# Attention: weights' gains and low parts, and the norm of keys and queries, on GpSimd; V's copies out of PSUM on ScalarE

## The chip, the core and the metric

The kernel runs on one core of one Trainium2 chip. A core has five engines that run side by side, each through its own list of instructions: TensorE (PE in the profile; its weight loads are PEld), VectorE (DVE), ScalarE (ACT), GpSimd (POOL) and SyncE (SP), which issues the DMAs here. They wait for one another by semaphores. The metric is the time of one execution on the device, in microseconds (us); less is better.

## What is computed

A trunk of two layers on 1024 tokens of width 1024, in float32. Layer one is a Mamba-2 mixer, layer two an attention mixer with 16 heads of 64; each is followed by a gated embedding. The change touches the attention alone. Cut to that, and with its helpers' names, the reference says:

```python
kv = rmsnorm(h, norm_g) @ w_kv
k = rmsnorm(kv[..., :SB_WIDTH].reshape(bsz, s, SB_HEADS, SB_HEAD_DIM), k_g)
v = kv[..., SB_WIDTH:].reshape(bsz, s, SB_HEADS, SB_HEAD_DIM)
...
qg = rmsnorm(h, norm_g) @ w_in
q = rmsnorm(qg[..., :SB_WIDTH].reshape(bsz, s, SB_HEADS, SB_HEAD_DIM), q_g)
z = jnp.einsum('bhtd,bhsd->bhts', q, k)
weights = jnp.where(strict, jnp.exp(jax.nn.log_sigmoid(z) + suffix), 0.0)
o = jnp.einsum('bhts,bhsd->bhtd', weights, v)
return (o * jax.nn.silu(gate)) @ w_out
```

`suffix` is the running sum of log_sigmoid(-z) over the later keys of a strictly causal row, and `rmsnorm` divides by the root of the mean square. The kernel holds the tokens in reverse order, turns the sums of logarithms into running products of sigmoid(-z), and weights the differences of neighbouring rows of V with them.

## The kernel before, in words

**Precision.** A product of float32 matrices is made of three products of rounded parts: each operand is split into a high part (rounded) and a low part (the remainder). `hilo` (line 99) makes the two: the high part on ScalarE (L104), and the low part either on GpSimd (L106, without a gain) or in one operation on VectorE that also multiplies by a gain (L108).

**Pairs of heads.** Attention works on eight pairs of heads, `hp` = 0 to 7. `Pairs.load` (line 752) fetches a pair's weights in four transfers of 128x1024 (L758) and splits each into four pieces of 128x256: two of key and value columns, with the gain `kvn`, and two of query and gate columns, with `sn`. So a pair has 16 pieces. The weights of the next pair are made while the present one runs.

**Steps.** A pair has four steps, p = 3, 2, 1, 0, of two blocks of 128 tokens each. `step(i)` (line 992) writes out TensorE's order by hand, from three steps at once: it projects step i (`project`, 48 matmuls, and `gate` for p = 3 and 2), with pieces of the two steps before it in between: `flip` and `scores` of step i-1, `turn` and `product` of step i-2. The flip stands at half of step i's projections. All other engines' orders come from the framework's planner, which takes the instructions as the program issues them and puts each on its engine when it expects its operands to be ready, the earlier issued first.

**What a step does around the change.** `project` (line 812) leaves key, value and query of a block in PSUM; L825 copies key and query out on ScalarE, L826 the value on VectorE. When both blocks are done, `step` calls `values` and then `norm` (lines 1028 and 1029).

`values` (line 843) needs V shifted by one row: L847 to L849 move it from partition to partition by DMA from SyncE's queue, L852 fetches its first rows. Then GpSimd subtracts (L853) and makes high and low parts for the two heads (L858, L859, twice each).

`norm` (line 861) squares key and query on ScalarE (L864), sums over 64 on VectorE (L867), forms the mean (L85), guesses the inverse root by integer operations (L74, L75), refines it three times (L77, L78, L79: three operations each, on 128x8) and multiplies key and query by it (L870, 128x512), all on VectorE. `flip` (line 873) transposes the result on TensorE (L879), and L885 to L890 split it for `scores`.

Of the kernel before, what the change touches and what calls it, by code (L numbers as in the profile page):

```python
# [8 lines left out]
F32 = mybir.dt.float32  # L9
F32R = mybir.dt.float32r  # L10
BF16 = mybir.dt.bfloat16
I32 = mybir.dt.int32
AF = mybir.ActivationFunctionType
ALU = mybir.AluOpType
# [4 lines left out]
P = 128  # L19
# [10 lines left out]
EPS = 1e-6  # L30
# [18 lines left out]
def split3_some(nc, out, pairs, m):  # L49

    n = len(pairs)
    for i, (a, b) in enumerate(pairs):
        nc.tensor.matmul(out, lhsT=a, rhs=b, start=(i == 0), stop=(i == n - 1))  # L53
        if i % m == m - 1 and i < n - 1:
            yield


def terms(a, b):
    return [(a[0], b[0]), (a[0], b[1]), (a[1], b[0])]
# [530 lines left out]
class PleWeights:  # L590
# [7 lines left out]
    def load(self, pool, n):  # L598

        k, layer = self.k, self.layer  # L600
        for kk in (0, 2, 4, 6, 8):
            src, j, out = (self.A["gate"], kk, self.gates) if kk < 8 else (self.A["proj"], 0, self.projs)
            raw = self.rawp.tile([P, 1024], F32, name="raw").rearrange("p (r c) -> p r c", c=512)
            k.nc.sync.dma_start(raw, src[layer, j * P:(j + 2) * P, n * 512:n * 512 + 512].rearrange("(r p) c -> p r c", p=P))
            for r in range(2):
                hi = pool.tile([P, 512], F32R, name=f"g{n}h")
                lo = pool.tile([P, 512], F32R, name=f"g{n}l")
                k.hilo(hi, lo, raw[:, r], k.plen[:, layer, kk + r:kk + r + 1] if kk < 8 else 0.5)
                out[j + r][n] = (hi, lo)
            yield  # L610
# [133 lines left out]
class Pairs:  # L744
# [7 lines left out]
    def load(self, hp):  # L752

        k = self.k
        st = self.sts[hp] = {"W": [], "hp": hp}
        for q in range(4):
            raw = self.rawp.tile([P, 1024], F32, name="raw")
            k.nc.sync.dma_start(raw, self.A["w_b"][hp, :, q * 1024:(q + 1) * 1024])  # L758
            pool, bufs = (self.pool, 10) if hp == 0 or (4 * hp + q) % 6 != 3 else (self.more, 2)
            for i in range(2):  # L760
                hi = pool.tile([P, 512], F32R, name="g0h", bufs=bufs)
                lo = pool.tile([P, 512], F32R, name="g0l", bufs=bufs)
                for m in range(2):
                    g = (k.kvn if m == 0 else k.sn)[:, 2 * q + i:2 * q + i + 1]
                    sl = slice(m * 256, m * 256 + 256)
                    k.hilo(hi[:, sl], lo[:, sl], raw[:, i * 512 + m * 256:i * 512 + m * 256 + 256], gain=g)
                st["W"].append((hi, lo))
            yield

# [14 lines left out]
def attention(k, A, rawp, hT, oTd, dbg, b2, pairs):  # L784


    tc, nc = k.tc, k.nc
# [3 lines left out]
    with ExitStack() as ctx:  # L791
        pp = ctx.enter_context(tc.tile_pool(name="b_pair", bufs=1, reuse_waits="tile"))
        wk = ctx.enter_context(tc.tile_pool(name="b_work", bufs=2, reuse_waits="tile"))
        sm = ctx.enter_context(tc.tile_pool(name="b_small", bufs=2, reuse_waits="tile"))
        zp = ctx.enter_context(tc.tile_pool(name="b_z", bufs=2, space=PSUM, reuse_waits="tile"))
        trp = ctx.enter_context(tc.tile_pool(name="b_tr", bufs=2, space=PSUM, reuse_waits="tile"))
        op = ctx.enter_context(tc.tile_pool(name="b_o", bufs=2, space=PSUM, reuse_waits="tile"))
# [14 lines left out]
        def project(st, b):  # L812
            W = st["W"]
            ps = mm.tile([P, 512], F32, name="mm")
            prs = []
            sl = slice(b % 4 * P, b % 4 * P + P)
            for kk in range(KT):
                whi, wlo = W[kk]
                prs += terms((hh[b // 4][:, kk, sl], hl[b // 4][:, kk, sl]), (whi[:, :384], wlo[:, :384]))
            yield from split3_some(nc, ps[:, :384], prs, 6)  # L820
            p = b // 2
            if b % 2:
                st["kq"] = wk.tile([P, 2, 2, P], F32, name="kq", bufs=2)
                st["vr"][p] = wk.tile([P, 2, P], F32, name="vr", bufs=3)
            nc.scalar.copy(st["kq"][:, b % 2], ps.rearrange("p (m c) -> p m c", c=256)[:, :, 0:128])  # L825
            nc.vector.tensor_copy(st["vr"][p][:, b % 2], ps[:, 128:256])  # L826
            yield

        def gate(st, half):
# [31 lines left out]
        def norm(st, p):  # L861
            kq = st.pop("kq")
            sq = wk.tile([P, 512], F32, name="sg", bufs=1)
            nc.scalar.activation(sq, kq.rearrange("p b m c -> p (b m c)"), AF.Square)  # L864
            n = 8
            ss = sm.tile([P, n], F32, name="kss")
            nc.vector.reduce_sum(ss, sq.rearrange("p (g d) -> p g d", d=64), axis=AX.X)  # L867
            y = k.rstd(sm, ss, n, 64, EPS, "kr")
            x = kq.rearrange("p b m (h d) -> p (b m h) d", d=64)
            nc.vector.tensor_tensor(x, x, y.unsqueeze(2).broadcast_to([P, n, 64]), op=ALU.mult)  # L870
            st["kn", p] = kq

        def flip(st, p):
# [98 lines left out]
        n = len(steps)  # L972
# [19 lines left out]
        def step(i):  # L992
# [12 lines left out]
            if i < n:  # L1005
                hp, p = steps[i]
                if p == NT // 2 - 1:
                    pairs.all(hp)
                    begin_pair(sts[hp])
                    if hp + 1 < 8:  # L1010
                        pairs.start(hp + 1)
                    else:
                        b2.begin(pairs)
                fill = [(project(sts[hp], 2 * p + 1), 5)]
                if p >= 2:
                    fill.append((gate(sts[hp], p - 2), 7))
                fill.append((project(sts[hp], 2 * p), 5))
# [7 lines left out]
            if i < n:  # L1025
                if p in LOADS:
                    pairs.step(hp + 1)
                values(sts[hp], p)
                norm(sts[hp], p)
                if i in CHUNKS:  # L1030
                    b2.weights(CHUNKS[i])
# [228 lines left out]
```

## Time and profile before

| | |
|---|---|
| median of three runs | 1833.93 us (1831.68 to 1837.17) |
| the profiled execution's own time | 1837.69 us |
| its span in the trace | 1836.0 us |
| TensorE busy | 1725.0 us, 94% of the span |
| VectorE, ScalarE, GpSimd busy | 1189.7, 894.6, 402.2 us |
| attention stage | from about 930 to about 1600 us of the span |

The span is what the trace covers; the own time has the start and the end of the execution around it. Busy time counts an engine's instructions, not its waits. In the views, a line such as L853 is the line of the kernel that issued the instruction, `out<-in` are the program's tiles, and what stands behind "<-" at the end of a row is what ended the idle time ahead of it. SPq is the queue of SyncE that issues DMAs: its duration is that of the issue, not of the transfer. The granted clock is the share of TensorE's full clock that it was given, 1.00 being 2.4 GHz and 0.50 being 1.2 GHz.

### The profile page before, as it was taken

How to read it: one execution, taken by the hardware profiler on the slowest of the kernel's cores; microseconds unless marked ns; L12 is line 12 of the kernel's file. 1: busy time of each engine (PE TensorE's matmuls, PEld its weight loads, DVE VectorE, ACT ScalarE, POOL GpSimd, SP SyncE). 2: the span in 40 equal slices, each digit the busy share in tenths (PEclk: the TensorE clock that was granted, in tenths of full speed). 3: DMA queues.
4: the chain of work that ended last, by engine and by line, in shares of the span. 5: the costliest groups of instructions: out<-in, count | busy, mean ns of one | idle time of the engine just before them, and what ended most of it. 6: DMA issues, size and time to landing. Idle time of an engine off the chain costs nothing.

```text
span 1836.0 us, 25269 instructions
## 1 busy us (share of the span) xinstructions
PE 1725.0 (94%) x9170; PEld 1452.7 (79%) x9170; DVE 1189.7 (65%) x2462; ACT 894.6 (49%) x1910; POOL 402.2 (22%) x448
## 2 busy tenths in 40 slices
PE   7999999999999999999998999899999998689999
PEld 6777877877876787888887888788888887578887
DVE  6687278279169554345658797887878787962332
ACT  6567359349337332124436564564646554641221
POOL 0234534524625122200001011111101011210110
PEclk9999999999999999999999999999999999899999
DMA  4223213213212754322212010101111012232110
GB/s 155 66 81 91 82 62 94 90 60 99 92 52 87 238 160 149 118 97 78 94 40 65 19 54 19 52 31 39 44 29 65 19 44 74 87 118 69 51 38 35
DMA packets 96397, 139.42 MB, mean 76 GB/s; under 512 B 18160, under 2 KB 66640, under 8 KB 96272
## 3 DMA queue, kind: packets, MB, share of 16 engines
q1 hardware_dynamic: 96272, 137.80, 23.4%
q8 instruction: 72, 1.18, 0.3%
q14 instruction: 53, 0.43, 0.1%
HBM read 108.77 MB, written 24.77 MB: 73 GB/s over the span
## 4 chain that ended last, share of the span: by engine, by line
PE 67%; DVE 20%; ACT 7%; DMA 3%; issue 2%; POOL 0%; SPq 0%; DVEq 0%; ACTq 0%
PE mm L46 40%; PE mm L53 12%; DVE pt L910 6%; PE pq L46 2%; PE oq L942 2%; DVE v L234 2%; PE intra L409 2%; DVE g0l L108 1%; PE tr L922 1%; DVE wl L932 1%; PE inter L404 1%; ACT pt L908 1%; PE tr L664 1%; DMA raw<-in_gate 1%; PE tr L925 1%
## 5 line engine op out<-in xcount | busy, mean ns | idle before, releaser
L46 PE MATMUL mm<-ul,wh 128*128 128x512 f32 (+1 forms) x648 | 254.0, 392 | 0.0
L46 PE MATMUL mm<-uh,wh 128*128 128x512 f32 (+1 forms) x648 | 252.6, 390 | 0.8 <-ACT v L232 0.7
L46 PE MATMUL mm<-uh,wl 128*128 128x512 f32 (+1 forms) x648 | 252.5, 390 | 0.0
L53 PE MATMUL mm<-g0h,hh 128*128 128x384 f32 x512 | 182.7, 357 | 0.0
L910 DVE TENSOR_TENSOR_SCAN pt<-pt,keep 128x128 f32<-128x128 f32 (+7 forms) x128 | 177.0, 1386 | 0.8 <-ACT pt L908 0.3
L53 PE MATMUL mm<-g0l,hh 128*128 128x384 f32 x512 | 172.8, 337 | 2.4 <-DVE g0l L108 2.4
L53 PE MATMUL mm<-g0h,hl 128*128 128x384 f32 x512 | 172.9, 338 | 0.0
L234 DVE SCALAR_TENSOR_TENSOR v<-u,convh,v 128x512 f32<-128x512 f32 x144 | 129.4, 904 | 53.5 <-ACT v L232 51.0
L931 ACT CAST wh<-tr 128x512 fp32r<-128x512 f32 (+1 forms) x160 | 86.9, 544 | 154.8 <-PE tr L925 154.0
L853 POOL TENSOR_TENSOR vs<-vs,vr 128x256 f32<-128x256 f32 x32 | 24.1, 754 | 550.3 <-DMA vs<-vr 319.1
L46 PEld LDWEIGHTS mm<-uh,wh 128*128 128x128 f32 x648 | 121.7, 188 | 26.9 <-ACT v L232 1.6
L46 PEld LDWEIGHTS mm<-ul,wh 128*128 128x128 f32 x648 | 121.7, 188 | 26.3 <-issue 2.3
L46 PEld LDWEIGHTS mm<-uh,wl 128*128 128x128 f32 x648 | 121.8, 188 | 25.8 <-issue 1.9
L932 DVE TENSOR_TENSOR wl<-tr,wh 128x512 fp32r<-128x512 f32 (+1 forms) x160 | 101.5, 635 | 43.8 <-ACT wh L931 41.6
L106 POOL TENSOR_TENSOR wl<-raw,wh 128x1024 fp32r<-128x1024 f32 x39 | 95.3, 2444 | 157.6 <-ACT wh L104 150.9
L922 PE MATMUL tr<-ident,pt 128*128 128x128 f32 x320 | 75.4, 284 | 31.5 <-DVE wl L932 28.9
L574 DVE SCALAR_TENSOR_TENSOR acc<-mm,rg,acc 128x512 f32<-128x512 f32 x64 | 47.8, 749 | 84.9 <-PE mm L46 83.5
L53 PEld LDWEIGHTS mm<-g0l,hh 128*128 128x128 f32 x512 | 96.9, 189 | 4.0 <-DVE g0l L108 3.0
L906 PE MATMUL z<-kst,qh 128*128 128x320 f32 (+3 forms) x192 | 72.9, 380 | 27.9 <-ACT pt L908 15.8
L53 PEld LDWEIGHTS mm<-g0h,hh 128*128 128x128 f32 x512 | 96.6, 189 | 1.0
L53 PEld LDWEIGHTS mm<-g0h,hl 128*128 128x128 f32 x512 | 96.4, 188 | 0.0
L647 DVE SCALAR_TENSOR_TENSOR pth<-pth,pq 128x512 f32<-128x512 f32 (+1 forms) x33 | 22.2, 672 | 113.8 <-PE pq L46 109.1
(350 smaller groups left out, 4356.8 us busy)
## 6 DMA issues: line engine op xcount, KB each, us to landing
raw<-in_w_in SPq DMA_DIRECT2D x40, 512.0 KB
ex<-acd SPq DMA_DIRECT2D x64, 256.0 KB
raw<-in_w_b SPq DMA_DIRECT2D x32, 512.0 KB
raw<-in_m_out SPq DMA_DIRECT2D x16, 512.0 KB
raw<-in_gate SPq DMA_DIRECT2D x16, 512.0 KB
graw<-gT SPq DMA_DIRECT2D x30, 256.0 KB
gT<-zs SPq DMA_DIRECT2D x28, 256.0 KB
acc<-in_x SPq DMA_DIRECT2D x8, 512.0 KB
```

Of the source, the lines that this page charges most:

```text
L46: nc.tensor.matmul(out, lhsT=a, rhs=b, start=(i == 0), stop=(i == n - 1))
L53: nc.tensor.matmul(out, lhsT=a, rhs=b, start=(i == 0), stop=(i == n - 1))
L106: (eng or nc.gpsimd).tensor_tensor(lo, raw, hi.bitcast(F32), op=ALU.subtract)
L234: nc.vector.scalar_tensor_tensor(vv, u[:, 3 - j:3 - j + 512], w(j), vv, op0=ALU.mult, op1=ALU.add)
L409: nc.tensor.matmul(aq[hp * 64:hp * 64 + 64, jp * 256 + i * P:jp * 256 + (i + 1) * P], lhsT=xdts[2 * qt + i][:, (2 * j + hp) * 64:(2 * j + ...
L574: nc.vector.scalar_tensor_tensor(acc[:, sl], ps, k.rg[:, g, t:t + 1], acc[:, sl], op0=ALU.mult, op1=ALU.add)
L906: nc.tensor.matmul(z[:, :n], lhsT=qh[:, h, qs], rhs=rk, start=True, stop=False)
L910: nc.vector.tensor_tensor_scan(pt[:, :N], pt[:, :N], keep[:, :N], 1.0, op0=ALU.mult, op1=ALU.max)
L922: nc.tensor.transpose(tq[:, c:c + P], al[:, i0:i0 + P], ident)
L931: nc.scalar.copy(wh[:, :c], tq[:, :c])
L932: nc.vector.tensor_tensor(wl[:, :c], tq[:, :c], wh[:, :c].bitcast(F32), op=ALU.subtract)
L942: nc.tensor.matmul(out[:, :w], lhsT=st["V"][j // 2][:, j % 2, h * P:(h + 1) * P], rhs=rhs, start=(j0 == 2 * p and i == 0), stop=(j0 == NT ...
```

## The change

Three parts. For pairs 1 to 7 a piece of the weights is first multiplied by its gain in place on GpSimd, and then split without a gain: high part on ScalarE, low part on GpSimd instead of VectorE. Pair 0 is left as it was. The copy of V out of PSUM goes to ScalarE. In the norm the three refinements, written as four operations each, and the product with key and query go to GpSimd; mean and first guess stay on VectorE.

```diff
@@ -763,7 +763,12 @@
                 for m in range(2):
                     g = (k.kvn if m == 0 else k.sn)[:, 2 * q + i:2 * q + i + 1]
                     sl = slice(m * 256, m * 256 + 256)
-                    k.hilo(hi[:, sl], lo[:, sl], raw[:, i * 512 + m * 256:i * 512 + m * 256 + 256], gain=g)
+                    x = raw[:, i * 512 + m * 256:i * 512 + m * 256 + 256]
+                    if hp == 0:
+                        k.hilo(hi[:, sl], lo[:, sl], x, gain=g)
+                    else:
+                        k.nc.gpsimd.tensor_scalar(x, x, g, None, op0=ALU.mult)
+                        k.hilo(hi[:, sl], lo[:, sl], x)
                 st["W"].append((hi, lo))
             yield
 
@@ -823,7 +828,7 @@
                 st["kq"] = wk.tile([P, 2, 2, P], F32, name="kq", bufs=2)
                 st["vr"][p] = wk.tile([P, 2, P], F32, name="vr", bufs=3)
             nc.scalar.copy(st["kq"][:, b % 2], ps.rearrange("p (m c) -> p m c", c=256)[:, :, 0:128])
-            nc.vector.tensor_copy(st["vr"][p][:, b % 2], ps[:, 128:256])
+            nc.scalar.copy(st["vr"][p][:, b % 2], ps[:, 128:256])
             yield
 
         def gate(st, half):
@@ -865,9 +870,17 @@
             n = 8
             ss = sm.tile([P, n], F32, name="kss")
             nc.vector.reduce_sum(ss, sq.rearrange("p (g d) -> p g d", d=64), axis=AX.X)
-            y = k.rstd(sm, ss, n, 64, EPS, "kr")
+            v, y, r = (sm.tile([P, n], F32, name=x) for x in ("krv", "kry", "krs"))
+            nc.vector.tensor_scalar(v, ss, 1.0 / 64, EPS, op0=ALU.mult, op1=ALU.add)
+            nc.vector.tensor_single_scalar(y.bitcast(I32), v.bitcast(I32), 1, op=ALU.logical_shift_right)
+            nc.vector.tensor_scalar(y.bitcast(I32), y.bitcast(I32), -1.0, float(0x5F3759DF), op0=ALU.mult, op1=ALU.add)
+            for _ in range(3):
+                nc.gpsimd.tensor_tensor(r, y, v, op=ALU.mult)
+                nc.gpsimd.tensor_tensor(r, r, y, op=ALU.mult)
+                nc.gpsimd.tensor_scalar(r, r, -0.5, 1.5, op0=ALU.mult, op1=ALU.add)
+                nc.gpsimd.tensor_tensor(y, r, y, op=ALU.mult)
             x = kq.rearrange("p b m (h d) -> p (b m h) d", d=64)
-            nc.vector.tensor_tensor(x, x, y.unsqueeze(2).broadcast_to([P, n, 64]), op=ALU.mult)
+            nc.gpsimd.tensor_tensor(x, x, y.unsqueeze(2).broadcast_to([P, n, 64]), op=ALU.mult)
             st["kn", p] = kq
 
         def flip(st, p):
```

## Rows read from the trace of the kernel before

**Rows 1.** The page, busy time of TensorE: us, share of the span, instructions.

```profile
PE 1725.0 (94%) x9170; PEld 1452.7 (79%) x9170; DVE 1189.7 (65%) x2462; ACT 894.6 (49%) x1910; POOL 402.2 (22%) x448
```

**Rows 2.** Windows, one pair each: us, PE, PEld, DVE, ACT, POOL busy, clock, DMA.

```profile
1152.36:1234.04 81.68, 75.12 (x456) 68.57 (x456) 67.50 (x151) 46.75 (x107) 9.42 (x20) 1.00 0.13 39
1234.04:1318.45 84.41, 77.80 (x456) 70.78 (x456) 67.60 (x151) 46.73 (x107) 9.42 (x20) 0.96 0.12 38
```

**Rows 3.** Waits, attention stretch: total us, times, longest us.

```profile
PE tr L922 <- DVE wl L932: 28.9, 22, 5.2
PE z L906 <- ACT qh L889: 12.1, 9, 3.6
```

**Rows 4.** Groups by line (busy us, mean ns; idle before), VectorE and ScalarE.

```profile
L108 DVE SCALAR_TENSOR_TENSOR g0l<-raw,kvn,g0h 128x256 fp32r<-128x256 f32 x64 | 32.7, 511 | 0.4
L826 DVE COPY vr<-mm 128x128 f32<-128x128 f32 x64 | 18.2, 285 | 10.0 <-ACT kq L825 9.5
L825 ACT COPY kq<-mm 128x256 f32<-128x256 f32 x64 | 23.8, 372 | 38.0 <-PE mm L53 37.6
L78 DVE SCALAR_TENSOR_TENSOR krs<-krs,kry 128x8 f32<-128x8 f32 x96 | 20.9, 218 | 1.4
L870 DVE TENSOR_TENSOR kq<-kq,kry 128x512 f32<-128x512 f32 x32 | 22.0, 689 | 0.8
```

**Rows 5.** Timeline, steps p = 2, 1, 0 of one pair: start us, us.

```profile
1204.30 0.64 SPq L847 DMA_DIRECT2D vs<-vr  x1
1204.50 0.69 DVE L867 TENSOR_REDUCE kss<-sg 128x8 f32<-128x512 f32 x1 [0.23 <-ACT sg L864]
1209.02 0.69 DVE L870 TENSOR_TENSOR kq<-kq,kry 128x512 f32<-128x512 f32 x1
1210.99 0.27 PE L879 MATMUL tr<-ident,kq 128*128 128x128 f32 x1
1212.36 0.74 POOL L853 TENSOR_TENSOR vs<-vs,vr 128x256 f32<-128x256 f32 x1 [25.01 <-DMA vs<-vr]
1213.16 0.53 POOL L858 CAST V<-vs 128x128 fp32r<-128x128 f32 x2
1213.65 0.88 POOL L859 TENSOR_TENSOR V<-vs,V 128x128 fp32r<-128x128 f32 x2
1217.05 0.65 SPq L847 DMA_DIRECT2D vs<-vr  x1
1225.50 0.33 PE L879 MATMUL tr<-ident,kq 128*128 128x128 f32 x1
1234.67 0.67 SPq L847 DMA_DIRECT2D vs<-vr  x1
1249.06 0.38 PE L879 MATMUL tr<-ident,kq 128*128 128x128 f32 x2
```

**Rows 6.** Groups of GpSimd (busy us, mean ns; last line min/median/max ns).

```profile
L393 POOL TENSOR_TENSOR st<-st,decay 128x512 f32<-128x512 f32 x24 | 31.5, 1311 | 64.5 <-DVE st L394 46.0 <-ACT st L391 18.5
L853 POOL TENSOR_TENSOR vs<-vs,vr 128x256 f32<-128x256 f32 x32 | 24.1, 754 | 550.3 <-DMA vs<-vr 319.1 <-DVE krs L78 74.2 <-PE mm L53 63.5
L858 POOL CAST V<-vs 128x128 fp32r<-128x128 f32 x64 | 20.3, 345 | 2.1
L229 POOL MEMSET u<- 128x3 f32 x24 | 2.4, 101 | 4.1 <-DVE v L234 4.1
L231 POOL COPY u<-u x24: 181/187/782, 29.8 to 534.6; 128x3 f32<-128x3 f32 x24
```

**Rows 7.** Timeline, then a window (clock after the busy times): a late flip.

```profile
1589.87 0.45 PE L879 MATMUL tr<-ident,kq 128*128 128x128 f32 x1 [4.45 <-DVE kq L870]
1589.80:1592.80 3.00, 2.79 (x12) 2.53 (x12) 1.94 (x3) 1.86 (x4) 0.00 (x0) 0.50 0.80 244
```

**Rows 8.** Timeline, GpSimd and VectorE at one moment near the end.

```profile
1582.77 2.49 POOL L106 TENSOR_TENSOR hl<-raw,hh 128x1024 fp32r<-128x1024 f32 x1
1582.95 2.33 DVE L78 SCALAR_TENSOR_TENSOR krs<-krs,kry 128x8 f32<-128x8 f32 x1
```

## The prediction

> **What bounds the kernel now.** I read the page first: TensorE counts as busy for 94% of the span [rows 1], so whatever is taken off another engine is worth at most the idle time of TensorE that this other engine causes. The change touches the attention stage alone, so next I cut that stage into windows, one for each head pair, with the borders at the same instruction (the end of the pair's last L825 copy). An undisturbed pair takes 81.68 us, of which TensorE is busy for 75.12 [rows 2]: 6.56 us of idle a pair, some 52 us over the eight pairs. VectorE is busy for 67.50 us of the pair, ScalarE for 46.75, GpSimd for 9.42 [rows 2]. So the engine that is relieved is the fullest one behind TensorE, and the one that is loaded is nearly empty. The view of the waits says what TensorE idles for: its transposes wait for VectorE's low part `wl` (28.9 us in all), and its scores for ScalarE's `qh` copies, which stand behind VectorE in the chain of the flip (12.1 us) [rows 3].
>
> That view does not show what an operand's lateness would cost, since it lists only what is late today. So I read the timeline of one pair around the norm. In step p = 2 the DMA of the shifted V (L847) is issued at 1204.30, the norm's sum starts on VectorE at 1204.50, the normalised key and query are done at 1209.02 + 0.69 = 1209.71, and TensorE transposes them (the flip, L879) at 1210.99: a margin of 1.28 us. GpSimd's first operation on the shifted V, L853, starts at 1212.36, that is 8.06 us behind the issue of L847, which it waits for; its casts and subtractions last until 1213.65 + 0.88 = 1214.53 [rows 5]. The reader is to see that L853 starts after the flip that the same step's norm has to serve. GpSimd stood idle for 550.3 us ahead of the 32 L853 [rows 6]: that idle time is waiting in the queue, not free time for whatever is listed behind it.
>
> **The change, part by part.** All sums are against the profiled execution's own 1837.69 us (span 1836.0 and 1.69 around it), 3.76 above the median of the three runs; at the end I take that off.
>
> *Off VectorE.* Seven pairs of 16 low parts are 112 x 0.511 = 57 us; 64 V copies x 0.285 = 18 us; 32 norms lose nine small operations at 0.22 or less and a product of 0.689, that is 32 x 2.6 = 84 us [rows 4]. That is about 20 us of the 67.5 in a pair. It is worth only what ends TensorE's idle time. I take 2.5 of the 6.56 us: about half of the waits for `wl` (28.9 / 8 = 3.6 a pair), and half of those for `qh` (1.5 a pair). Eight pairs: -20 us; ends 0 and -52 (all idle time gone).
>
> *V's copies on ScalarE.* One half of L825 in size, whose copy takes 0.372; between 0.285 and 0.372 [rows 4]. It comes straight behind L825, so L847 is issued about 0.2 us earlier than now, and the square 0.3 us later, which lies beside the 8 us of the DMA. Nothing counted but those 0.2; if it delayed a sigmoid that TensorE waits for each time, 64 x 0.37 = 24 us.
>
> *The weights on GpSimd.* 112 products in place and 112 subtractions of 128x256. The subtraction has L853's shape, 0.754; the product, of one input, lies between the cast's 0.345 for half as many and 0.754; I take 0.45 [rows 6]. That is 19 us a pair, and no bound by itself: with today's 9.4 and the norms' 14 GpSimd is busy for 43 of 82 us. The product needs only the raw weights, which are loaded long before; the low part is hidden as long as it is there before the next pair's first projection. I count nothing; if half of a pair's 16 subtractions stood behind a late norm, 8 x 0.754 = 6 us a pair, 42 over seven.
>
> *The norm on GpSimd.* Twelve operations of 128x8 and a product of 128x512. No row of before has such a small product on GpSimd: between the 0.101 of a memset and the 0.345 of the 128x128 cast; I take 0.19, by the copy of 128x3, the nearest in size, with a median of 0.187. So 2.3 us (1.2 to 4.1), and the large product 1.3, as L393 [rows 6]. By itself that would fit. But `values` is called ahead of `norm` in each step, and both now issue on GpSimd. What is queued behind L853's wait is the whole chain, and who waits for the chain is the flip, on TensorE, whose order is written by hand. I take it that L853 stands ahead of the chain's end: the chain is then ready 8.1 (the DMA) + 2.2 (L853 to the end of V) + 2.3 + 1.3 = 13.9 us behind L847, 13.7 behind where L847 is issued now. The flip comes 1210.99 - 1204.30 = 6.69 us behind L847 for p = 2, 1225.50 - 1217.05 = 8.45 for p = 1, 1249.06 - 1234.67 = 14.39 for p = 0 [rows 5]; p = 3 is followed by the pair's longest step, so I count nothing there. TensorE waits for 7.0 and 5.3 us, and not for p = 0: 12.3 us a pair, 98 over eight. With the chain's ends: 10.1 us a pair at 1.2, and 8.8 + 7.1 + 1.1 = 17.0 at 4.1, so 81 and 136.
>
> *The clock.* Once in the trace a flip was late: TensorE idled for 4.45 us and then ran with a granted clock of 0.50, the lower level, for the next 3 us [rows 7]. A pair in which the clock's mean fell to 0.96 took 84.41 instead of 81.68, 2.7 us more [rows 2]. Sixteen late flips, each longer than that, at 1.6 us (what half a clock costs in some 3 us) are +26; ends 0 and 16 x 2.7 = 43.
>
> **A rule weighed.** VectorE's L78, which takes 0.218 us in the mean, took 2.33 when it met GpSimd's L106 of 2.49 us [rows 4, 8]: an operation of VectorE with two operands in SBUF ended only with GpSimd's. The Trainium skill says so as a rule (GPSIMD Engine Reference, section Specifications): GpSimd shares its SBUF interfaces with VectorE, with contention where VectorE has two SBUF inputs. By that row the change adds 112 x 0.754 + 32 x 1.3 = 126 us of such GpSimd work against which VectorE's scans and GpSimd's chain would queue; I leave it out of the likeliest sum, since during a late flip VectorE runs out of work, and make a rival of it.
>
> That GpSimd takes nothing ahead of a waiting instruction is what the forecast hangs on, and in the trace of before everything behind L853 depends on it, so no row proves it. The Trainium skill (TensorE: Matmul & The Clock Gate, section on the array being 16 of 32x32) calls GpSimd's queue strictly first in, first out; no run here shows it yet.
>
> **The sum.** 1837.7 - 20 + 98 + 26 = 1941.7 by the profile's own time; less 3.8, **1938 us** by the median, 5.7% slower.
>
> **The rivals.**
> *The chain is listed ahead of L853 (faster).* The planner orders GpSimd by what it expects to be ready, and the norm's inputs come soon: L867 starts 0.2 us behind L847 [rows 5]. The sum of 0.69 and three small operations, then 3.6 on GpSimd, put the product some 5.2 us behind L847, 1.5 ahead of the flip at 6.69. From there on TensorE never waits for it, and only the relief is left: -20 to -52, so 1782 to 1814, say 1800. For it: GpSimd is nearly empty. Against it: all thirteen operations have to come first; one behind L853 is enough to make the flip late, and the call order puts L853 first.
> *The same, and given back.* The flip is in time, but ScalarE's additional copies (up to 24 us) and GpSimd's share of the port eat the relief: 1834 within 5.
> *The port stretches the chain.* L853 first, and in addition each of the chain's nine two-operand products queues behind a scan of VectorE, at 0.2 to 0.3 us each: the chain is ready at 16 instead of 13.7. TensorE then waits 9.3 + 7.6 + 1.6 = 18.5 us a pair, 148 over eight; with 26 for the clock and no relief beyond 15, about 1993.
>
> **How the numbers follow.** Forecast 0.70; port rival 0.15; chain ahead 0.10; given back 0.05. The forecast's own range, from the chain's ends, the clock's ends and the relief's: 1834 + 81 - 40 = 1875 to 1834 + 136 + 43 - 10 = 2003. For 8 in 10 I leave out the two rivals that end faster or the same (0.15) and the far end above 1995. Faster by over 0.3% (about what a measurement of this kernel can tell from no change, as its three runs lie within that) 0.10; within 0.3% 0.05; slower 0.85.
>
> **What would show it.** Right: GpSimd's chain operations lie behind L853 in the timeline, L879 has idle time ended by GpSimd's product (L870's successor), about 7 and 5 us long, twice a pair; the granted clock falls to 0.5 behind them; a pair takes some 95 us; VectorE's busy time is down by about 159 us and GpSimd's up by about 250. Wrong: L879 has no idle time, because the chain's last product ends before L853 starts; then the pair is shorter than 81.7 us and the first rival holds. The sum is off in size if the wait of L853 is no longer 8 us, if the small operations are not near 0.19, or if the projections wait for `g0l` from GpSimd, which I counted at nothing.

## The result, and the profile after

The changed kernel takes 2002.8 us in the median (2001.85 to 2005.27) against 1833.24 beside it: 1.0916 of the time before, 95% interval 1.0898 to 1.0933. That is 170 us slower; 104 had been forecast. The profiled execution took 2002.18 us, its span is 2000.5, so against the profile of before 164.5 us have to be found.

The new lines of the change move what stands behind them: L847 is now L852, the V subtraction L853 is L858, its casts and low parts L863 and L864, the chain's four operations L878 to L881, its product L883, the flip L892. L770 is the weights' product with the gain, the low part `wl` is L945.

The page of after: busy times (against [rows 1]), then the chain that ended last, by line.

```profile
PE 1761.8 (88%) x9170; PEld 1491.8 (75%) x9170; DVE 1067.7 (53%) x1966; ACT 893.2 (45%) x1974; POOL 717.3 (36%) x1088
...
PE mm L46 38%; PE mm L53 10%; DMA vs<-vr 8%; PE pq L46 2%; DVE v L234 2%; POOL raw L770 2%; PE intra L409 2%; PE oq L955 2%; PE tr L892 1%; DVE pt L923 1%; POOL g0l L106 1%; POOL kq L883 1%; PE inter L404 1%; PE tr L935 1%; POOL V L864 1%
```

VectorE has lost 122 us and GpSimd gained 315 (159 and 250 had been forecast). GpSimd's excess is the weights' product with the gain, 131 us in all in place of 50; on VectorE the durations added up fell by 151, but they overlap in the trace. TensorE does the same 9170 matmuls and is busy for 36.8 us more: that is the clock. And a DMA of 127 KB, the shift of V, is now 8% of the chain that sets the end.

The waits of after: total us, times, longest us.

```profile
POOL vs L858 <- DMA vs<-vr: 239.2, 24, 17.5
...
PE tr L892 <- POOL kq L883: 146.2, 24, 11.3
PE tr L935 <- DVE wl L945: 19.7, 10, 4.9
...
PE mm L46 <- ACT kst L104: 12.8, 1, 12.8
...
PE mm L53 <- POOL g0l L106: 6.6, 2, 3.6
```

The flip waits for GpSimd's product, 24 times; before, it was late twice, both in the last pair: 1.36 us in p = 2 and 4.45 in p = 0 [rows 7]. `wl` fell from 28.9 us [rows 3] to 19.7: the relief of VectorE is there. The wait for `kst` lies behind the attention, at the end.

The windows of after: one pair, then the step that holds p = 2's projections and the three behind it.

```profile
1217.27:1319.72 102.45, 80.30 (x458) 73.81 (x456) 52.43 (x87) 46.34 (x115) 52.40 (x105) 0.90 0.10 32
...
1249.17:1275.65 26.48, 24.13 (x153) 22.02 (x151) 17.47 (x26) 12.90 (x30) 5.68 (x18) 1.00 0.03 6
1275.65:1296.06 20.41, 14.25 (x83) 13.77 (x82) 7.37 (x18) 6.76 (x20) 5.74 (x18) 0.83 0.10 33
1296.06:1319.72 23.66, 17.08 (x92) 16.21 (x91) 10.60 (x21) 12.03 (x33) 13.25 (x29) 0.86 0.14 40
1319.72:1351.60 31.88, 24.83 (x137) 21.81 (x136) 17.00 (x24) 14.66 (x37) 27.74 (x40) 0.89 0.14 45
```

The pair takes 102.45 us, 20.77 more than the 81.68 of [rows 2]. TensorE is busy for 5.18 us of these (80.30 against 75.12, the clock), and idle for 15.59 more (22.15 against 6.56). The three steps behind the first hold the late flips, of p = 2, 1 and 0 in this order, and the clock is below 1.00 in each of them.

The timeline of the same stretch, GpSimd's instructions with SyncE's issue, VectorE's scans and the three flips between them: start us, us, then at the end the idle time ahead and what ended it.

```profile
1275.85 0.64 SPq L852 DMA_DIRECT2D vs<-vr  x1
1278.16 0.20 POOL L878 TENSOR_TENSOR krs<-kry,krv 128x8 f32<-128x8 f32 x1 [13.86 <-DVE kry L876]
...
1279.33 0.23 POOL L881 TENSOR_TENSOR kry<-krs,kry 128x8 f32<-128x8 f32 x1
1283.97 0.72 POOL L858 TENSOR_TENSOR vs<-vs,vr 128x256 f32<-128x256 f32 x1 [4.41 <-DMA vs<-vr]
1284.65 0.20 POOL L878 TENSOR_TENSOR krs<-kry,krv 128x8 f32<-128x8 f32 x1
...
1288.08 1.04 POOL L883 TENSOR_TENSOR kq<-kq,kry 128x512 f32<-128x512 f32 x1
1289.18 1.11 PE L892 MATMUL tr<-ident,kq 128*128 128x128 f32 x4 [6.16 <-POOL kq L883]
...
1304.33 0.74 POOL L858 TENSOR_TENSOR vs<-vs,vr 128x256 f32<-128x256 f32 x1 [15.21 <-DMA vs<-vr]
...
1306.44 0.20 POOL L878 TENSOR_TENSOR krs<-kry,krv 128x8 f32<-128x8 f32 x1
1306.72 0.20 POOL L879 TENSOR_TENSOR krs<-krs,kry 128x8 f32<-128x8 f32 x1
...
1309.82 1.04 POOL L883 TENSOR_TENSOR kq<-kq,kry 128x512 f32<-128x512 f32 x1
1310.92 1.11 PE L892 MATMUL tr<-ident,kq 128*128 128x128 f32 x4 [5.99 <-POOL kq L883]
...
1318.44 0.92 POOL L770 TENSOR_SCALAR raw<-raw,sn 128x256 f32<-128x256 f32 x1
1319.18 1.49 DVE L923 TENSOR_TENSOR_SCAN pt<-pt,keep 128x640 f32<-128x640 f32 x1
1319.34 2.06 POOL L770 TENSOR_SCALAR raw<-raw,kvn 128x256 f32<-128x256 f32 x1
1321.39 2.44 POOL L770 TENSOR_SCALAR raw<-raw,sn 128x256 f32<-128x256 f32 x1
1321.43 1.75 DVE L923 TENSOR_TENSOR_SCAN pt<-pt,keep 128x768 f32<-128x768 f32 x1
...
1333.59 0.20 POOL L878 TENSOR_TENSOR krs<-kry,krv 128x8 f32<-128x8 f32 x1
1333.75 0.73 POOL L106 TENSOR_TENSOR g0l<-raw,g0h 128x256 fp32r<-128x256 f32 x1
1334.44 0.20 POOL L879 TENSOR_TENSOR krs<-krs,kry 128x8 f32<-128x8 f32 x1
...
1339.78 1.04 POOL L883 TENSOR_TENSOR kq<-kq,kry 128x512 f32<-128x512 f32 x1
1340.88 1.11 PE L892 MATMUL tr<-ident,kq 128*128 128x128 f32 x4 [6.23 <-POOL kq L883]
```

Three flips, three delays of 6 us. In p = 2 GpSimd does four of the chain's thirteen operations and then stands still for 4.41 us, because L858 is next in its list and the shifted V lands 8.12 us behind its issue at 1275.85. The other nine wait behind it, though nothing of theirs is missing. In p = 1 all thirteen stand behind it. In p = 0 the chain shares the queue with the weights: from 1333.59 on, each of its first five small operations is followed by a subtraction (L106) of 0.73 us, and others of the weights stand around V's operations just before.

### The profile page after: what moved, and what is told of

The parts are those of the page before. It is cut to its first block, busy times and chain, and to the rows that moved or that the text cites. A ratio compares the mean times of both kernels' runs of the same rounds, so it can differ in the third digit from the quotient of the medians.

```text
span 2000.5 us, 25655 instructions
## 1 busy us (share of the span) xinstructions
PE 1761.8 (88%) x9170; PEld 1491.8 (75%) x9170; DVE 1067.7 (53%) x1966; ACT 893.2 (45%) x1974; POOL 717.3 (36%) x1088
## 4 chain that ended last, share of the span: by engine, by line
PE 62%; POOL 10%; DMA 10%; DVE 9%; ACT 5%; issue 4%; POOLq 0%; SPq 0%; DVEq 0%; ACTq 0%
PE mm L46 38%; PE mm L53 10%; DMA vs<-vr 8%; PE pq L46 2%; DVE v L234 2%; POOL raw L770 2%; PE intra L409 2%; PE oq L955 2%; PE tr L892 1%; DVE pt L923 1%; POOL g0l L106 1%; POOL kq L883 1%; PE inter L404 1%; PE tr L935 1%; POOL V L864 1%
## 5 line engine op out<-in xcount | busy, mean ns | idle before, releaser
L53 PE MATMUL mm<-g0h,hh 128*128 128x384 f32 x512 | 194.3, 379 | 0.0
L53 PE MATMUL mm<-g0l,hh 128*128 128x384 f32 x512 | 183.2, 358 | 6.6 <-POOL g0l L106 6.6
L53 PE MATMUL mm<-g0h,hl 128*128 128x384 f32 x512 | 182.3, 356 | 0.0
L892 PE MATMUL tr<-ident,kq 128*128 128x128 f32 x128 | 31.1, 389 | 146.2 <-POOL kq L883 146.2
L945 DVE TENSOR_TENSOR wl<-tr,wh 128x512 fp32r<-128x512 f32 (+1 forms) x160 | 100.7, 637 | 105.7 <-ACT wh L944 103.6
L106 POOL TENSOR_TENSOR wl<-raw,wh 128x1024 fp32r<-128x1024 f32 x39 | 95.2, 2442 | 155.8 <-ACT wh L104 155.8
L899 DVE SCALAR_TENSOR_TENSOR kst<-tr,gkq,kst 64x256 fp32r<-64x256 f32 x64 | 30.9, 483 | 211.1 <-ACT kst L898 210.0
L892 PEld LDWEIGHTS tr<-ident,kq 128*128 128x128 f32 x128 | 20.6, 195 | 153.4 <-POOL kq L883 153.3
L858 POOL TENSOR_TENSOR vs<-vs,vr 128x256 f32<-128x256 f32 x32 | 24.8, 776 | 266.3 <-DMA vs<-vr 239.2
L898 ACT ACTIVATE kst<-tr,gkq 64x256 fp32r<-64x256 f32 x64 | 30.0, 469 | 201.2 <-PE tr L892 196.2
L53 PEld LDWEIGHTS mm<-g0l,hh 128*128 128x128 f32 x512 | 104.9, 205 | 8.2 <-POOL g0l L106 7.2
L53 PEld LDWEIGHTS mm<-g0h,hh 128*128 128x128 f32 x512 | 105.2, 206 | 1.1
L53 PEld LDWEIGHTS mm<-g0h,hl 128*128 128x128 f32 x512 | 104.4, 204 | 0.0
```

The costliest lines, as they stand in the source:

```text
L106: (eng or nc.gpsimd).tensor_tensor(lo, raw, hi.bitcast(F32), op=ALU.subtract)
L892: nc.tensor.transpose(tq[:, m * 256 + i * P:m * 256 + (i + 1) * P], kn[:, i, m], ident)
L899: nc.vector.scalar_tensor_tensor(kst[x, h, tsl], kt[o], g, kst[o, h, tsl].bitcast(F32), op0=ALU.mult, op1=ALU.subtract)
L945: nc.vector.tensor_tensor(wl[:, :c], tq[:, :c], wh[:, :c].bitcast(F32), op=ALU.subtract)
```

## The experiments

Ratios are to the kernel before, run beside each experiment, with 95% intervals. "Norm", "weights" and "V" name the three parts of the change; a part that isn't moved is as before.

**The parts one by one.** *Norm alone* (the last hunk of the change, cut here).

```diff
-            y = k.rstd(sm, ss, n, 64, EPS, "kr")
...
+                nc.gpsimd.tensor_tensor(r, y, v, op=ALU.mult)
...
-            nc.vector.tensor_tensor(x, x, y.unsqueeze(2).broadcast_to([P, n, 64]), op=ALU.mult)
+            nc.gpsimd.tensor_tensor(x, x, y.unsqueeze(2).broadcast_to([P, n, 64]), op=ALU.mult)
```

> Only the norm's refinements and product go to GpSimd; weights and V's copies as before. Theory A (the norm's chain is listed behind the subtraction that waits for V's DMA): the flips of p = 2 and p = 1 come about 6 us late, those of p = 0 at most 1 us, since no pieces of weights stand in the chain; 8 x (12 + twice 1.7 for the clock) = +105 to 125 us, so 1940 to 1960 us. Theory B (the moved weights are what costs): the flips are nearly in time, under 1880 us. Theory C (the chain itself is too slow on GpSimd, wherever it stands): as A in time, which the kernel with the chain listed first tells apart.

Measured: 1971.69 us, 1.0751 (1.0735 to 1.0767). The norm by itself makes 138 of the 170 us. Its page gives TensorE 1757.8 us busy, 32.8 more than before. From its waits, the flips:

```profile
PE tr L887 <- POOL kq L878: 124.7, 25, 10.8
```

Its span is 134.1 us over that of before. The clock is 32.8; the flips are 124.7 less the 5.8 us of two that were late before, one of them in [rows 7], so 118.9; then 17.6 us are won elsewhere. In one pair the flips are 5.60, 7.11 and 0.96 us late. p = 0's is late by 1, not by 6. The time is 12 us above theory A's range all the same: the first pair's p = 3 flip is late too, by 4.34 us, and the last pair's three by 10.76, 6.16 and 6.81.

*Weights and V, without the norm* (the first two hunks).

```diff
+                        k.nc.gpsimd.tensor_scalar(x, x, g, None, op0=ALU.mult)
+                        k.hilo(hi[:, sl], lo[:, sl], x)
...
-            nc.vector.tensor_copy(st["vr"][p][:, b % 2], ps[:, 128:256])
+            nc.scalar.copy(st["vr"][p][:, b % 2], ps[:, 128:256])
```

> Weights on GpSimd and V's copies on ScalarE as in the change; the norm stays on VectorE as before. Theory A: no flip is late by more than 2 us; 1815 to 1845 us. Theory B: the projections or the flips of p = 0 wait for GpSimd in each pair; over 1870 us.

Measured: 1856.55 us, 1.0124 (1.0109 to 1.0139). Neither theory had it: no flip is late but two of the last pair, and still the kernel is 23 us slower. So I took the two parts apart.

*V alone* (the second hunk).

```diff
-            nc.vector.tensor_copy(st["vr"][p][:, b % 2], ps[:, 128:256])
+            nc.scalar.copy(st["vr"][p][:, b % 2], ps[:, 128:256])
```

> Only the copies of V go to ScalarE. Theory A (the copies are nearly free; the moved weights are what made the run with weights and V's copies 1856.6): 1828 to 1838, no change that can be measured, the shift of V issued about 0.2 us earlier. Rival (ScalarE's 64 more copies delay the sigmoids and cause those 23 us): 1845 to 1858.

Measured: 1855.08 us, 1.0111 (1.0073 to 1.0148), the four runs from 1844.85 to 1860.63. Theory A falls: a copy of 0.27 us, which I had costed at nothing, makes 20 us. The rival has the time, but its reason covers a small part: in the profiled execution, whose span is 15.9 us longer, the scores' waits for the sigmoids rise from 15.8 to 19.7 us. The larger parts are TensorE's busy time, that is the clock (1734.4 against 1725.0), and the last pair's p = 2 flip, late by 8.71 in place of 1.36 us; the waits for `wl` rise by 4.5, those for `qh` fall by 5.2. Why that flip is later was not tried. On the clock, here is, in the timeline of the kernel before, TensorE's longest wait of a pair, in two pairs:

```profile
1187.61 0.33 PE L922 MATMUL tr<-ident,pt 128*128 128x128 f32 x1 [2.72 <-DVE wl L932]
1269.25 0.47 PE L922 MATMUL tr<-ident,pt 128*128 128x128 f32 x1 [2.69 <-DVE wl L932]
```

And its windows, the 4 us behind each (the clock is the third number from the end):

```profile
1188.00:1192.00 4.00, 4.00 (x25) 3.41 (x24) 2.77 (x8) 1.18 (x2) 0.00 (x0) 1.00 0.01 0
1270.00:1274.00 4.00, 4.00 (x14) 3.32 (x12) 2.16 (x5) 0.59 (x1) 0.00 (x0) 0.50 0.02 0
```

The timeline of the same place with V's copies on ScalarE, with GpSimd's V subtraction and VectorE's L77 just before it, and the window behind it:

```profile
1274.50 0.86 POOL L853 TENSOR_TENSOR vs<-vs,vr 128x256 f32<-128x256 f32 x1 [22.12 <-DMA vs<-vr]
1274.76 0.63 DVE L77 TENSOR_TENSOR krs<-kry,krv 128x8 f32<-128x8 f32 x1
1277.57 0.48 PE L922 MATMUL tr<-ident,pt 128*128 128x128 f32 x1 [2.98 <-DVE wl L932]
```

```profile
1278.00:1282.00 4.00, 4.00 (x15) 3.42 (x14) 2.23 (x5) 0.59 (x1) 0.00 (x0) 0.50 0.02 0
```

In the kernel before, a wait of 2.7 us for `wl` is followed by the full clock in one pair and by 0.50 in another. With V's copies the wait is 2.98, and four pairs in a row, the fourth to the seventh, have a mean clock of 0.96 and take 85.3 us each; before, the same four took between 81.58 and 84.41, and one of them had a clock of 0.96 [rows 2]. What makes it longer is, as I read the timeline, the very thing that I had booked as a small gain: V's shift is issued earlier, so GpSimd's subtraction meets VectorE's chain ahead of `wl` and holds L77 for 0.63 us. That link was not tested by itself, and before the subtraction holds another operation of VectorE at this place (L959, 0.86 us in place of 0.34), so it is no more than a guess.

*Weights alone* (the first hunk).

```diff
-                    k.hilo(hi[:, sl], lo[:, sl], raw[:, i * 512 + m * 256:i * 512 + m * 256 + 256], gain=g)
...
+                        k.nc.gpsimd.tensor_scalar(x, x, g, None, op0=ALU.mult)
+                        k.hilo(hi[:, sl], lo[:, sl], x)
```

> Only the weights' products and low parts go to GpSimd. Theory A: 1850 to 1862, all of what the run with weights and V's copies lost, and TensorE's clock falls in more pairs than the two of before, since VectorE's scans end later and the low part wl with them. Rival (V's copies cost it): 1828 to 1838.

Measured: 1854.72 us, 1.0112 (1.0092 to 1.0132), as A had it. The first pair whose weights GpSimd makes takes 92.19 us in place of 83.48, of which 4.8 is one wait for `g0l`; the pairs behind the next one win 1.4 us in p = 0's step and lose 2.0 to 2.6 in p = 3's, where the clock now falls. The two parts do not add up (19 and 20, together 23); why was not tried.

**Order or wait?** *Chain first*: the change with `norm` called ahead of `values`, and an edge in the planner that puts the V subtraction behind the norm's product on GpSimd.

```diff
-                values(sts[hp], p)
                 norm(sts[hp], p)
+                values(sts[hp], p)
...
-            nc.gpsimd.tensor_tensor(vs, vs, vr, op=ALU.subtract)
+            sub = nc.gpsimd.tensor_tensor(vs, vs, vr, op=ALU.subtract)
+            tc.add_manual_dep(sub.ins, st["np"].ins.name, mybir.DependencyInfo(
+                mybir.DependencyClass.NoSync, mybir.DependencyReason.SCHED_ONLY), reason="chain first")
...
-            nc.gpsimd.tensor_tensor(x, x, y.unsqueeze(2).broadcast_to([P, n, 64]), op=ALU.mult)
+            st["np"] = nc.gpsimd.tensor_tensor(x, x, y.unsqueeze(2).broadcast_to([P, n, 64]), op=ALU.mult)
```

> The changed kernel with one difference in order: the norm is called ahead of V's shift, and an ordering edge puts the subtraction that waits for V's DMA behind the norm's product in GpSimd's list. No work is added or taken away. Theory A: the product ends some 6 us behind the second copy of key and query for p = 2 and 1, and those flips (7.2 and 9.1 us behind it) are in time; at p = 0 the pieces of weights still stand in the chain, so up to 3 us late; 1810 to 1860 us. Theory C: the flips of p = 2 and 1 stay late, over 1930 us.

Measured: 1880.92 us, 1.0258 (1.0242 to 1.0274): 122 us less than the change with the same instructions, and 21 above theory A's range, since p = 0's flip is later than the 3 us that it allowed. The timeline of one pair, flips of p = 2, 1, 0:

```profile
1320.38 0.66 PE L894 MATMUL tr<-ident,kq 128*128 128x128 f32 x4
1335.83 0.66 PE L894 MATMUL tr<-ident,kq 128*128 128x128 f32 x4 [1.12 <-POOL kq L885]
1364.58 1.11 PE L894 MATMUL tr<-ident,kq 128*128 128x128 f32 x4 [5.56 <-POOL kq L885]
```

p = 2 is in time, p = 1 almost, p = 0 is not. A pair takes 88.5 us, 8 more than the 80.6 of the run below that leaves the weights on VectorE and has this flip in time; 3.1 of these are TensorE's busy time, the clock (77.95 against 74.82 in the windows).

*No wait*: the change with the V subtraction reading V twice in place of the shifted V. Its place ahead of the chain is kept, only the wait for the DMA is gone.

```diff
-            nc.sync.dma_start(vs[0:P - 1], vr[1:P])
+            nc.sync.dma_start(vd[0:P - 1], vr[1:P, :, 0:8])
...
-            nc.gpsimd.tensor_tensor(vs, vs, vr, op=ALU.subtract)
+            nc.gpsimd.tensor_tensor(vs, vr, vr, op=ALU.subtract)
```

> The changed kernel with the V subtraction reading V itself in place of the shifted V, so that it waits for no DMA (the transfers are still issued, into a small tile that nobody reads, and of 8 columns only; V's shift is left out of the result). Its place ahead of the chain in GpSimd's queue stays. Theory A (what costs is the 8 us of waiting at the head of GpSimd's queue, not the order as such, nor GpSimd's own work): the flip of p = 2 is less than 1 us late, that of p = 1 less than 2, that of p = 0 stays 5 to 6 late by the weights; 1875 to 1900, as where the chain stood first (1880.9). Rival (GpSimd's load and its share of the port with VectorE hold the chain whatever it waits for): p = 2 and p = 1 stay over 3 us late, 1930 or more.

Measured: 1905.19 us, 1.0389 (1.0367 to 1.0411). p = 2 is 0.5 and p = 1 is 1.4 us late, as theory A had it; p = 0 is 7.0 instead of 5 to 6, which puts the time 5 us above its range. So about 98 of the 170 us are the waiting at the head of GpSimd's queue; about 24 more went with the order in *chain first*. The rival falls: GpSimd has the same operations here, and shares with VectorE what it shared before.

**What makes p = 0 late.** The change with the weights' low parts back on VectorE, the products still on GpSimd.

```diff
-                        k.hilo(hi[:, sl], lo[:, sl], x)
+                        k.hilo(hi[:, sl], lo[:, sl], x, eng=k.nc.vector)
```

> The changed kernel with the weights' low parts back on VectorE (the products stay on GpSimd). Theory A (the flip of p = 0 is 6.25 us late because the weights' subtractions stand one by one between the operations of the norm's chain in GpSimd's queue): the flip of p = 0 comes down to 1 to 2 us late, as in the run with the norm alone, and the time to 1965 to 1985. Rival B (the products, which take up to 2.4 us beside VectorE's scans and push the V subtraction from 8.3 to 10.25 us, are what makes it late): p = 0 stays over 4 us late, 1992 to 2005.

Measured: 1980.48 us, 1.0797 (1.0778 to 1.0815). The flips of one pair, p = 2, 1, 0:

```profile
1376.53 1.11 PE L892 MATMUL tr<-ident,kq 128*128 128x128 f32 x4 [6.16 <-POOL kq L883]
1398.88 1.11 PE L892 MATMUL tr<-ident,kq 128*128 128x128 f32 x4 [6.74 <-POOL kq L883]
1424.34 0.66 PE L892 MATMUL tr<-ident,kq 128*128 128x128 f32 x4 [0.31 <-POOL kq L883]
```

p = 0 falls from 6.23 to 0.31 us late (1.66 at most in another pair but the last): the subtractions in and ahead of the chain made it late. The long products did not; they are still there. The last pair is another matter. Its p = 0 flip comes when no further pair's weights are made, and it is as late here as in the change (the change first, then this run):

```profile
1747.43 1.12 PE L892 MATMUL tr<-ident,kq 128*128 128x128 f32 x4 [5.92 <-POOL kq L883]
1725.13 1.12 PE L892 MATMUL tr<-ident,kq 128*128 128x128 f32 x4 [5.93 <-POOL kq L883]
```

The time falls by 22 us, less than the flips of p = 0 do, because those of p = 1 rise from 6.0 to 6.7 us late.

**What is left to win.** *Chain first, without the weights* (norm and V moved).

```diff
-                        k.nc.gpsimd.tensor_scalar(x, x, g, None, op0=ALU.mult)
-                        k.hilo(hi[:, sl], lo[:, sl], x)
+                    k.hilo(hi[:, sl], lo[:, sl], raw[:, i * 512 + m * 256:i * 512 + m * 256 + 256], gain=g)
```

> As the kernel with the chain listed first, but with the weights' low parts on VectorE as before. Theory A: no flip late, and what is left of the relief of VectorE shows: 1795 to 1830 us. If relief of VectorE is worth nothing to TensorE, 1830 to 1840. Theory C: over 1930 us.

Measured: 1830.64 us, 0.9978 (0.9967 to 0.9989), where the first two ranges meet. With the weights on GpSimd as well it was 1880.92, so in this order the weights cost 50 us. From the third to the seventh, the pairs run at the full clock and take 80.56 us each, 1.1 less than an undisturbed pair before. The kernel was 13 us ahead where the last pair's projections end (1558.5 against 1571.8), and 7 at the end of the span. *Norm alone, chain first*: the same with V's copies on VectorE.

```diff
-            nc.scalar.copy(st["vr"][p][:, b % 2], ps[:, 128:256])
+            nc.vector.tensor_copy(st["vr"][p][:, b % 2], ps[:, 128:256])
```

> Only the norm on GpSimd, with its chain ahead of the V subtraction; weights and V's copies as before. Theory A (V's copies on ScalarE cost by delaying the sigmoids ahead of the low part wl, 20 us where VectorE is not relieved): the norm moved in the right order gains more without them than the 1830.6 with them, 1815 to 1828. Rival (with the norm off VectorE that delay is covered, and VectorE now has to make the copies in its place): 1829 to 1840.

Measured: 1830.39 us, 0.9982 (0.9972 to 0.9992), as the rival had it. A pair takes 80.3 us here. Two more kernels put the norm of p = 1 back on VectorE.

```diff
+            if p == 1:
+                y = k.rstd(sm, ss, n, 64, EPS, "kr")
...
+            else:
```

With V moved:

> Chain first, V's copies on ScalarE, weights as before, and the norm of p = 1 back on VectorE, where the chain on GpSimd was 1.18 us late. Theory A: no flip is late but two in the last pair; 7 or 8 times 1.2 us less than the 1830.6 of the run with all four norms moved: 1815 to 1824, 0.5 to 1% faster than before. Rival (given back to the waits behind: the low part wl and the end's wait for kst): 1828 to 1834.

Measured: 1833.33 us, 0.9991 (0.9981 to 1.0001). With V as before:

> The same, with the norm of p = 1 on VectorE as before. Theory A (the 1.2 us by which p = 1's flip is late on GpSimd is what is left to win): 1 to 8 us below the run beside it that moves all four norms. Rival (a flip in time moves the idle time to the scores' wait for qh and to TensorE's clock, as where V's copies had moved too: 1833.3 against 1830.6): the same as that run or up to 6 us above it.

Measured: 1831.61 us, 0.9982 (0.9973 to 0.9991). In both the p = 1 flip is in time, and nothing is won, the times are the rivals': the scores now wait for `qh` (5.7 and 7.5 us in all, 1.8 where all four norms are moved). With V moved the mean clock is 0.984 in place of 0.989 too; with V as before it is 0.986 and 0.987, no clear difference. Something else kept all four near 1831. It is seen in the waits of *norm alone, chain first* behind the last projections, of TensorE and of SyncE's queue:

```profile
PE mm L46 <- ACT kst L104: 12.5, 1, 12.5
...
SPq L1098 <- DVE g0l L108: 9.5, 2, 8.7
```

TensorE waits 12.5 us for the first operand of the output projection; before, that wait was 1.6 us. The operand comes by a DMA (L1098), which SyncE issues only when VectorE has split the next weights out of a buffer (L108). SyncE's wait for that does not tell the two kernels apart (before, it is 10.0 us in all, the longest 7.0), but the time of the issue does. Before, then in this kernel:

```profile
1597.23 7.81 SPq L1088 DMA_DIRECT2D raw<-oTd  x2
1596.17 1.69 SPq L1098 DMA_DIRECT2D raw<-oTd  x2
```

That is 25.5 us behind the end of the last pair's projections before (1571.77), and 38.0 here (1558.13). So the last pair was put back on VectorE:

```diff
+            if st["hp"] == 7:
+                y = k.rstd(sm, ss, n, 64, EPS, "kr")
...
+            else:
```

> Only the norm on GpSimd, chain first, for the pairs 0 to 6; the last pair's norm on VectorE as before. Theory A (each of the first pairs ends about 1.3 us earlier, 80.3 against 81.7, and what is won is lost again only in the last pair, by flips 5.3 and 4.2 us late, and behind it, in a wait of 12.5 us for kst): 1818 to 1826. Rival (the end of the kernel is set by something else, the buffer that SP's transfer of oTd waits for and VectorE's splits of the last weights ahead of it, so whatever the pairs win is given back there): 1828 to 1834.

Measured: 1824.43 us, 0.9944 (0.9923 to 0.9964). The wait for `kst` is gone, and the DMA is issued 25.4 us behind the last projections (at 1585.39, behind 1559.97); what in the moved norm of the last pair made it late was not tried by itself. The waits of this kernel:

```profile
PE mm L46 <- ACT kst L104: 1.6, 1, 1.6
```

This is within theory A's range. The version beats both kernels, 8 us below the one before: norm on GpSimd ahead of V's subtraction, for the first seven pairs alone.

## Why the prediction was wrong

The direction held, and so did the mechanism of p = 2 and p = 1. Their flips wait for a chain that stands behind a DMA in GpSimd's queue: without that wait 98 us came back, with the order changed 122. The sum against the profile, term by term, of 164.5 us:

| term | forecast | after |
|---|---|---|
| relief of VectorE, and all other idle time | -20 | -12.7 |
| flips of p = 2 and p = 1 | 98 | 102.6 |
| flip of p = 0 | 0 | 33.0 |
| flip of the first step | 0 | 4.8 |
| clock | 26 | 36.8 |
| sum | 104 | 164.5 |

The 24 late flips are 146.2 us. p = 0 has 37.5 of them (five of 6.2, one of 0.3 and, in the last pair, one of 5.9), the very first flip 4.8, and p = 2 and p = 1 the other 103.9. Of the 5.8 that were there before, 4.5 go off p = 0 and 1.4 off p = 2; "Once in the trace a flip was late" overlooked the second. The relief is what is left of the sum.

*The step that failed* is "The weights on GpSimd ... I count nothing", together with "not for p = 0". I asked only who waits for the weights, not what waits behind them. Who waits is little: TensorE waits for `g0l` twice, 6.6 us in all. But the subtractions stand inside and ahead of the chain of p = 0. In the five pairs where they do, its flips are 31.2 us late; with the subtractions back on VectorE these are late by 0.3 to 1.7 each. The last pair's 5.9, of which 4.5 were there before, is not theirs. With weights and V's copies added, the norm alone goes from 1971.69 to 2002.8, 31 us. The upper end that I wrote down, 42 us if half of a pair's subtractions stood behind a late norm, was near that with the order turned round. I took the other end, and left the 42 out of the range as well, although the flip of p = 0 had only 0.7 us to spare by my own numbers (13.7 against 14.39). Without p = 0's 33.0, and some 8 for the clock behind its five waits of 6.2 at 1.5 each (an estimate), the time would have been near 1960.

The range has a slip of its own: it takes the relief at 40 and 10, not at the ends of 52 and 0 that I had given it. With those it would be 1863 to 2013.

*The flips of p = 2 and 1.* Forecast 7.0 and 5.3, measured 6.16 and 5.99 in the pair shown. There the sum was right by luck, by two errors against each other. The small operations take 0.20 us each, as taken, but start 0.28 apart where each needs the one before it (1306.44, 1306.72), so twelve are 3.4 us, not 2.3; the product takes 1.04, not 1.3. In p = 2 four operations went ahead of L858, which gave a part of that back. Over all pairs the term is 4.6 over: the p = 2 flip is 8.0 us late in the first pair and 11.3 in the last. V's casts and low parts took as long as expected.

*The clock.* I took 16 late flips at 1.6 us. There are 24, at 1.5 (36.8 / 24, net of what some pairs had lost before; in the pair shown 5.18 / 3 = 1.7). The price held; the number fell short, mostly by those of p = 0.

*V's copies* I costed at nothing, with 24 us if they delayed each sigmoid. Alone they make 20 us, of which the sigmoids' waits are about 4. The largest part came by a way that was not on the list: the clock, at a wait of 2.7 us behind which it had fallen in some pairs already, as in the second of [rows 2].

*Relief.* The waits for `wl` fell by 9.2 us, and the wait for `kst` at the end rose from 1.6 to 12.8. Without that and what the waits for `g0l` grew by (2.4 to 6.6) the relief is -28, more than the -20. In the run of the norm alone it is -17.6, with a wait of 11.9 for `kst` in it.

*The rivals.* "The chain is listed ahead of L853" was forecast at 1782 to 1814. When I forced it, with all of the change, it gave 1880.9, and without the weights 1830.6: but for p = 1's 1.2 us and the last pair the flips were in time, and yet the relief was given back, much of it behind the last pair's projections, where a lead of 13 us shrank to 7. "The port stretches the chain" came nearest in time (1993), for a wrong reason: the chain's small operations take 0.20 to 0.22 us in the mean of the whole trace (the slowest, L879, stands in the last rows below), so they are hardly stretched. By the Trainium skill (SBUF — State Buffer, section Who interferes with whom) the pair of ports that GpSimd and VectorE share is an exclusive lock, and the order of issue decides who is held up. The trace agrees on the lock where both are busy: the product L770, 0.92 us by itself, takes 2.06 when it starts 0.16 behind a scan of 1.49, and 2.44 beside one of 1.75. It does not settle the order: that second scan is listed 0.04 us behind the product that it holds up.

That GpSimd takes nothing ahead of a waiting instruction is now shown: the timeline's 4.41 us in p = 2, and the run without the wait. The Trainium skill (TensorE: Matmul & The Clock Gate, section on the array being 16 of 32x32) has it as a rule, and the trace agrees.

## What to carry to other kernels

Before an instruction is moved to another engine, write down that engine's list around it: what waits in front of it sets its time, and an idle engine that waits for a DMA is not free. Ask it also the other way, for each work that has no deadline of its own: whose short chain will it stand in? And where the clock falls behind the same wait in some pairs and not in others, expect the cost of small delays to be large: 0.3 us more of that wait went with 3.6 us a pair here against an undisturbed one, 2.7 of it TensorE's busy time.

## What I had not expected of the hardware

- GpSimd's product by a gain for each partition, 128x256, takes 0.92 us alone, longer than the two-operand subtraction of the same size (0.73). In the mean of the trace it is 1.08 and 1.26, where 0.45 had been forecast:

```profile
L106 POOL TENSOR_TENSOR g0l<-raw,g0h 128x256 fp32r<-128x256 f32 x112 | 84.8, 771 | 7.7 <-ACT g0h L104 7.7
L770 POOL TENSOR_SCALAR raw<-raw,sn 128x256 f32<-128x256 f32 x56 | 70.4, 1256 | 0.0
L770 POOL TENSOR_SCALAR raw<-raw,kvn 128x256 f32<-128x256 f32 x56 | 60.6, 1083 | 17.0 <-DMA raw<-in_w_b 17.0
L879 POOL TENSOR_TENSOR krs<-krs,kry 128x8 f32<-128x8 f32 x96 | 21.3, 222 | 5.9
```

- The product by the norm's factor, 128x512, takes 1.04, less than the 1.31 of L393 at that size [rows 6]: its second operand is 8 values, each used for 64 elements. The rows don't show whether that is the reason.
- The granted clock can be 1.00 or 0.50 behind waits of 2.72 and 2.69 us, in two pairs of one execution.
